# A hybrid encoder block on one core: up-projection of two chunks by seven block products in place of eight, behind the attention

## The chip, the core and the metric

The kernel runs on one core of a Trainium2 chip. The metric is the device time of one execution in microseconds (us); lower is better. TensorE (PE, with PEld for its weight loads) multiplies, VectorE (DVE), ScalarE (ACT) and GpSimd (POOL) do the elementwise work, and all transfers are issued from SyncE's queue (SP).

## What is computed

The reference takes x (2048 tokens of 1024 numbers, float32) through one encoder layer:

```python
hn = rms_norm(h, g_mix_pre)
u, q, k, v = split(hn @ w_in)                      # 512 wide each
mix = concat[pool_mixer(u), rms_norm(stick_breaking_attention(q, k, v)) * g_sb] @ w_out
h = h + rms_norm(mix, g_mix_post)
m = rms_norm(h, g_mlp_pre) @ w_up                  # 1024 -> 4096
m = square(relu(m)) @ w_down                       # 4096 -> 1024
h = h + rms_norm(m, g_mlp_post)
e = rms_norm(p @ w_ple_proj, g_ple)
h = h + sigmoid(h @ w_gate) * e
```

The attention is strictly causal: for each query, A = sigmoid(z) times the product of (1 - sigmoid(z)) over the keys between.

## The kernel before

**Tiling.** The tokens are cut into 4 chunks of 512. Activations lie feature-major: a tile has 128 features on the partitions and 512 tokens along the row. Every float32 operand of a product is split into a high part that PE reads exactly and a low rest (`split`, `pair`: an ACT copy and a DVE subtraction), and each product of 128 x 128 weights with 128 x 512 activations is three MATMULs (`mm3`): high by high, high by low, low by high. A weight tile is split at its first use and stored in DRAM as two halves; later chunks load those (`weight`, tiles `wh` and `wl`).

**Stages.** For each chunk: `ple` (p @ w_ple, its norm, tiles `e`), `prenorm`, `in_proj`, `u_proj` with `pool_mixer`, `attention`, `out_proj` with the residual (`output`), `feed_forward`, `gate`. The up-projection of one chunk (`mlp_ups`) makes 32 tiles of 128 hidden features, each from 8 x 3 MATMULs into one PSUM bank (tag `dn`); ACT takes the relu into `rl`, DVE squares it, and `pair` makes `m`. The down-projection (`mlp_downs`) takes two hidden tiles at a time (GF = 2): 8 output tiles of 6 MATMULs each (tag `dw`), which DVE adds into the page `acc`.

**Norms.** `add_square` squares a tile on ACT and adds it up on DVE (in `ple` on POOL) into `nrm`. `row_rstd` sums over the partitions with four small float32 matmuls against a column of ones (rows `nm<-ones,nrm`), makes the reciprocal root on POOL (`ms`), transposes it (`nm<-ident,rs`) and spreads it over the partitions by one more matmul (`nm<-rt,sel`).

**Attention.** A unit is one head and one pair of query and key chunk: 4 blocks of scores (`z`), two sigmoids on ACT (`q`, `pr`), a product scan on DVE (`q<-q,ones`), a product `pr<-pr,q` on POOL, 4 groups of transposes on PE (`tp`), their split (`at`: ACT and DVE), and 8 matmuls with the values (`op`). There are 80 units.

**Order.** The program is written twice. First the functions only record their operations, each with a due time: PE operations advance `plan.t`, the attention advances its own clock that runs `R_ATT` times as fast as its PE work. Then `Plan.order` simulates the engines with costs written by hand and fixes one order for each engine. On the chip each engine and the SP queue take their instructions in that order; what is late delays all that stands behind it. Buffers are 53 pages of SBUF and 8 PSUM banks.

**What runs beside what.** `attend` of chunks 0 to 3 is spread over the projections and the feed-forward of chunks 0, 1 and half of 2. `output(1)` is recorded within `feed_forward(0)`, `output(2)` within `feed_forward(1)`, `output(3)` within `feed_forward(2)`, `gate(0)` and `gate(1)` within `feed_forward(1)` and `(2)`. Behind `feed_forward(3)` come `gate(2)` and `gate(3)`. All recorded operations have the line of `Plan.record` (L275 in the profile), so rows are told apart by their tiles.

## Time and profile before

| | |
|---|---|
| median of 3 runs | 2663.43 us (2662.93 to 2663.47) |
| the profiled execution's own time | 2662.55 us |
| its span, first to last instruction | 2660.8 us |
| PE busy | 2626.7 us, 99% of the span |
| DVE / ACT / POOL busy | 64% / 39% / 27% |
| mean granted PE clock | 0.995 |
| moved by DMA | 668 MB, 251 GB/s |

PE's busy time is the first thing to look at, but its instructions are pipelined, so the time of a stretch is read from the distance of equal events in it, not from one instruction's duration. Idle time of an engine costs only where PE waits for it. In a group's row the mean duration of a DVE instruction contains what it waits for once it has started.

### The profile page before, as it was taken

Reading aid. Unit: us, or ns where it says so; the run is one execution under the profiler, and the core shown is the slowest. Engines: PE = TensorE matmul, PEld = TensorE weight load, DVE = VectorE, ACT = ScalarE, POOL = GpSimd, SP = SyncE. Lnnn points to the kernel's source line nnn. Section 1 sums busy time; section 2 is a strip of 40 time slices with the busy share of each in tenths; the row PEclk is TensorE's granted clock in tenths of the full one; section 3 lists DMA queues with packets and bytes.
Section 4 is the critical chain, followed back from the end, with each engine's and each line's share of the span. In section 5 each row is a group of like instructions: output and inputs, shape, how many; then the busy total and the mean of one; then the engine's idle time right before and its main releaser. Section 6 shows DMA issues by size and latency. Waiting matters only on the chain.

```text
span 2660.8 us, 34134 instructions
## 1 busy us (share of the span) xinstructions
PE 2626.7 (99%) x12312; PEld 2146.5 (81%) x12312; DVE 1709.8 (64%) x2331; ACT 1037.3 (39%) x1907; POOL 726.6 (27%) x663
## 2 busy tenths in 40 slices
PE   8999999999999999999999999999999999999999
PEld 6778787777888888888888888888887888888887
DVE  7854748868777759967665568685667273433454
ACT  8433536446445445445333343443334122111111
POOL 5432335344233323323333223333334000000000
PEclk9899999999999999999999999999999999999999
DMA  6899878878777758747955476475754675555576
GB/s 260 318 370 348 287 261 327 277 242 331 258 258 257 293 190 335 280 157 279 355 192 190 159 260 252 163 257 201 281 202 158 258 270 196 207 193 196 201 287 239
DMA packets 213129, 668.41 MB, mean 251 GB/s; under 512 B 22880, under 2 KB 39264, under 8 KB 212960
## 3 DMA queue, kind: packets, MB, share of 16 engines
q1 hardware_dynamic: 212960, 666.22, 69.8%
q8 instruction: 98, 1.61, 0.2%
q14 instruction: 71, 0.58, 0.1%
HBM read 489.97 MB, written 176.16 MB: 250 GB/s over the span
## 4 chain that ended last, share of the span: by engine, by line
PE 91%; DVE 4%; DMA 1%; ACT 1%; issue 1%; POOL 1%; SPq 0%; ACTq 0%; DVEq 0%; POOLq 0%
PE dn L275 50%; PE dw L275 26%; PE op L275 4%; PE z L275 4%; PE tp L275 4%; PE nm L275 2%; DVE q L275 1%; POOL nrm L275 1%; ACT nrm L275 1%; DMA wl<-d_w_up 0%; DMA d_y<-ypool 0%; DVE nrm L275 0%; DVE e L275 0%; DVE at L275 0%; POOL pt L275 0%
## 5 line engine op out<-in xcount | busy, mean ns | idle before, releaser
L275 PE MATMUL dn<-act,wh 128*128 128x512 f32 x2816 | 901.4, 401 | 4.3 <-ACT act L275 2.2
L275 POOL TENSOR_TENSOR pr<-pr,q 128x1 f32<-128x1 f32 (+4 forms) x512 | 564.5, 1115 | 1116.0 <-ACT pr L275 481.6
L275 PE MATMUL dw<-m,wh 128*128 128x512 f32 x2048 | 644.7, 396 | 3.0 <-DVE acc L275 3.0
L275 PEld LDWEIGHTS dn<-act,wh 128*128 128x128 f32 x2816 | 510.8, 190 | 103.0 <-issue 5.3
L275 PE MATMUL dn<-act,wl 128*128 128x512 f32 x1408 | 553.0, 393 | 0.0
L275 DVE TENSOR_TENSOR_SCAN q<-q,ones 128x512 f32<-128x512 f32 (+1 forms) x320 | 401.7, 1268 | 95.2 <-ACT q L275 94.0
L275 PEld LDWEIGHTS dw<-m,wh 128*128 128x128 f32 x2048 | 374.1, 188 | 76.3 <-DVE acc L275 3.4
L275 DVE TENSOR_TENSOR acc<-acc,dw 128x512 f32<-128x512 f32 x480 | 324.8, 681 | 139.1 <-PE dw L275 137.5
L275 PE MATMUL dw<-m,wl 128*128 128x512 f32 x1024 | 400.0, 391 | 0.0
L275 PEld LDWEIGHTS dn<-act,wl 128*128 128x128 f32 x1408 | 265.9, 189 | 57.8
L275 ACT CAST at<-tp 128x512 fp32r<-128x512 f32 (+1 forms) x320 | 166.5, 524 | 302.5 <-PE tp L275 271.9
L275 DVE TENSOR_TENSOR at<-tp,at 128x512 fp32r<-128x512 f32 (+1 forms) x320 | 191.1, 602 | 125.6 <-ACT at L275 125.2
L275 DVE TENSOR_TENSOR rl<-rl 128x512 f32<-128x512 f32 x128 | 97.7, 764 | 263.7 <-ACT rl L275 263.4
L275 ACT ACTIVATE q<-z 128x512 f32<-128x512 f32 (+1 forms) x320 | 171.3, 537 | 239.0 <-PE z L275 227.7
L275 ACT ACTIVATE rl<-dn 128x512 f32<-128x512 f32 x128 | 76.6, 598 | 472.3 <-PE dn L275 462.6
L275 PEld LDWEIGHTS dw<-m,wl 128*128 128x128 f32 x1024 | 192.2, 188 | 41.5
L275 POOL TENSOR_TENSOR ms<-ms,mhalf 128x4 f32<-128x4 f32 (+1 forms) x36 | 55.2, 1534 | 614.8 <-DVE ms L275 614.7
L275 PE MATMUL op<-at,kv 128*128 128x512 f32 (+3 forms) x640 | 182.9, 365 | 2.0 <-DVE at L275 2.0
L275 PE MATMUL z<-kv,qd 128*128 128x512 f32 (+3 forms) x640 | 178.1, 361 | 0.0
L275 ACT ACTIVATE pr<-z 128x512 f32<-128x512 f32 (+1 forms) x320 | 170.2, 534 | 5.2 <-PE op L275 2.6
L275 PE MATMUL tp<-ident,pr 128*128 128x128 f32 x1088 | 169.7, 272 | 1.2 <-DVE acc L275 0.6
L275 PEld LDWEIGHTS tp<-ident,pr 128*128 128x128 f32 x1088 | 136.0, 140 | 39.8 <-DVE acc L275 1.1
(118 smaller groups left out, 2961.7 us busy)
## 6 DMA issues: line engine op xcount, KB each, us to landing
wh<-d_w_up SPq DMA_DIRECT2D x96, 512.0 KB, 4.9
wl<-d_w_up SPq DMA_DIRECT2D x96, 512.0 KB, 6.0
wh<-d_w_down SPq DMA_DIRECT2D x96, 512.0 KB, 5.5
wl<-d_w_down SPq DMA_DIRECT2D x96, 512.0 KB, 5.2
xin<-d_h SPq DMA_DIRECT2D x48, 512.0 KB, 7.2
kv<-d_k SPq DMA_DIRECT2D x80, 256.0 KB, 6.1
kv<-d_v SPq DMA_DIRECT2D x80, 256.0 KB, 6.6
wh<-d_w_in SPq DMA_DIRECT2D x36, 512.0 KB, 8.1
```

What stands on the lines that cost most here:

```text
L275: fn(*[a.real() if isinstance(a, Ref) else a for a in args], **{k: a.real() if isinstance(a, Ref) else a for k, a in kw.items()})
```

## The change

`prenorm` no longer squares and adds the feature-major x. A second copy of x lies token-major in DRAM (`xr`, 4 tiles of 128 tokens x 1024 for each chunk); ACT squares each with a row sum (`token_sums`), so the four matmuls with ones go. In `ple` the sums move from POOL to DVE, and the scaling by gain and row norm moves to `gate`: the row norm is stored (`er`) and loaded there, and a gate tile takes three DVE operations in place of two. `output` of chunks 2 and 3 leaves the normalised activations unmade and hands on the row norm.

The feed-forward of chunks 2 and 3 is no longer interleaved with the attention. `output(2)` and `output(3)` lie within `feed_forward(1)`; then `moving_up` reads h1 of both chunks and makes 7 moving operands for each of 4 pairs of feature tiles (28 pages `xs`), beside `gate(0)`. `up_pair` then runs 16 times: it takes a 2 x 2 block (two halves of the features, two hidden tiles) against the 2 x 2 block (two halves of the features, two chunks), makes 4 sums of weights on DVE and splits them (`sa`, `so`), runs 7 products of 4 x 3 MATMULs and puts the four results together with one ACT copy and 7 DVE additions (`pu`, `mo`). The results are stored in DRAM and read back by `down_pair`, which takes both chunks and four hidden tiles at a time (GD = 4). `gate(1)`, `gate(2)`, `gate(3)` come last. The planner's numbers are others, and PE operations that read another engine's result are planned 2 us later (`MARGIN`).

```diff
+    def token_sums(self, rows):
+        sums = self.plan.tile([P, 16], F32, "ms")
+        for b in range(4):
+            t = self.plan.tile([P, D], F32, "xr")
...
+                self.sp.dma_start(out=t, in_=rows[b])
+            self.act.activation(t, t, AF.Square, accum_out=sums[:, b:b + 1])
...
+    def prenorm(self, dram, rows, which):
+        rs = self.rstd(self.token_sums(rows), 4, D)
         ts = [self.load2(dram, k2, "xp") for k2 in range(4)]
-        nrm = None
-        for k in range(NK):
-            nrm = self.add_square(nrm, ts[k // 2][:, k % 2, :])
-        r = self.row_rstd(nrm)
...
+            bank = self.spread(rs, self.bank("nm"))
...
-            nrm = self.add_square(nrm, m, self.pool)
-        r = self.row_rstd(nrm)
...
+            nrm = self.add_square(nrm, m)
...
+        self.sp.dma_start(out=dd["er"][c], in_=self.row_rstd(nrm))
...
+    def moving(self, k, b11, b12, b21, b22):
...
+        sub(t1, b12, b11)
+        sub(t2, b22, t1)
+        sub(t3, b22, b12)
+        sub(t4, b21, t2)
+        return [self.pair("xs", t) for t in (b11, b21, b22, t4, t1, t2, t3)]
...
+    def stationary_up(self, b, w_up, kept):
...
+        add(s1, a21, a22, ALU.add)
+        add(s2, s1, a11, ALU.subtract)
+        add(s3, a11, a21, ALU.subtract)
...
+        add(s4, a12, s2, ALU.subtract)
+        sums = [self.pair("so", t) for t in (s4, s1, s2, s3)]
...
+    def block(self, ws, xs, done):
...
+        p1 = mul(0)
...
+        self.act.copy(hold, p1)
+        u2 = add(hold, mul(5))
+        add(hold, mul(1), 0, 0)
+        u3 = add(u2, mul(6))
+        p5 = mul(4)
+        u4 = add(u2, p5)
+        add(u3, p5, 1, 1)
+        add(u4, mul(2), 0, 1)
+        add(u3, mul(3), 1, 0)
...
+    def down_pair(self, gi, accs, w_down, dd):
...
+            self.sp.dma_start(out=t, in_=dd["m"][gi * GD + j])
+            for i in range(2):
+                ms[i].append(self.pair("m", t[:, i, :]))
+        units = [self.weight(w_down[gi * GD + j], dd["w_down"][gi * GD + j], False) for j in range(GD)]
...
-                self.dve.tensor_tensor(out=s, in0=s, in1=ge[i][:, j, :], op=ALU.mult)
+                self.dve.scalar_tensor_tensor(out=s, in0=s, scalar=self.g(G_PLE, ot), in1=ge[i][:, j, :], op0=ALU.mult,
+                                              op1=ALU.mult)
+                self.dve.tensor_tensor(out=s, in0=s, in1=rows[i], op=ALU.mult)
                 self.dve.tensor_tensor(out=h, in0=h, in1=s, op=ALU.add)
...
-        feed_forward(1, ((G_GATE, gate, 0), (G_OUT, output, 2)))
-        feed_forward(2, ((G_GATE, gate, 1), (G_OUT, output, 3)))
+        feed_forward(1, ((G_OUT2, output, 2), (G_OUT3, output, 3)))
         plan.rate = 1.0
-        feed_forward(3, ())
+        xs = net.moving_up(2, 3, [acts[2], acts[3]])
+        gate(0)
+        for b in range(NF // 2):
+            net.up_pair(b, xs, w_up, dd)
+        accs = [[], []]
+        for gi in range(NF // GD):
+            net.down_pair(gi, accs, w_down, dd)
+        net.mlp_post(2, accs[0], dd)
+        net.mlp_post(3, accs[1], dd)
+        gate(1)
         gate(2)
-        plan.t += T_END
         gate(3)
-R_ATT = 4.515
+R_ATT = 3.117
+MARGIN = 2.0
...
-                        o.ready = max(o.ready, pick.end + LATENCY[e][o.engine])
+                        late = MARGIN if o.engine == "pe" and e != "pe" else 0.0
+                        o.ready = max(o.ready, pick.end + LATENCY[e][o.engine] + late)
```

What the change makes of the order is seen on three places. The first is PE at the program's start, where `pl` is the product p @ w_ple, `nm` a norm and `dn` the input projection. Before:

```order
L275 MATMUL pl<-pp,plew 128x512 x96
L275 MATMUL nm<-ones_76,nrm 128x1 x4
L275 MATMUL pl<-pp,plew 128x512 x6
L275 MATMUL nm<-ones_76,nrm 128x1 x4
L275 MATMUL pl<-pp,plew 128x512 x9
L275 MATMUL nm<-ident,rs 8x128
L275 MATMUL pl<-pp,plew 128x512 x6
L275 MATMUL nm<-rt,sel_92 128x512
```

The same place now:

```order
L279 MATMUL pl<-pp,plew 128x512 x48
L279 MATMUL nm<-ident,rs 8x128
L279 MATMUL pl<-pp,plew 128x512 x15
L279 MATMUL nm<-rt,sel_92 128x512
L279 MATMUL pl<-pp,plew 128x512 x12
L279 MATMUL nm<-ident,rs 8x128
L279 MATMUL pl<-pp,plew 128x512 x15
L279 MATMUL nm<-rt,sel_92 128x512
L279 MATMUL pl<-pp,plew 128x512 x36
L279 MATMUL nm<-ones_76,nrm 128x1 x4
```

The norms of x stand without their matmuls with ones and 48 `pl` MATMULs earlier; the first norm of `ple` now stands behind 126 of them.

The second is PE where the first gate (`dn<-actg`) begins; numbers tell the buffers apart. Before it stands among attention units (`z`, `tp`, `op`) and an up-projection (`dn<-act`):

```order
L275 MATMUL z_11528<-maskb_134,identb_129 128x128
L275 MATMUL dn_11484<-act_10252,wh_11152 128x512 x2
L275 MATMUL dn_11484<-act_10252,wl_11157 128x512
L275 MATMUL tp_11537<-ident_71,pr_11195 128x128 x2
L275 MATMUL tp_11537<-ident_71,pr_11244 128x128 x2
L275 MATMUL dn_11484<-act_10263,wh_11152 128x512 x2
L275 MATMUL dn_11484<-act_10263,wl_11157 128x512
L275 MATMUL op_11100<-at_11504,kv_10734 128x512 x2
L275 MATMUL dn_11484<-act_10274,wh_11152 128x512 x2
L275 MATMUL dn_11484<-act_10274,wl_11157 128x512
L275 MATMUL dn_11561<-actg_11404,wh_11393 128x512 x2
```

Now no attention is left there, and the end of that gate runs into the first of the seven products (`dn<-xs`):

```order
L279 MATMUL dn_17145<-actg_16825,wh_16957 128x512 x2
L279 MATMUL dn_17145<-actg_16825,wl_16970 128x512
L279 MATMUL nm_17134<-rt_17189,sel4_92 128x512
L279 MATMUL dn_17145<-actg_16835,wh_16957 128x512 x2
L279 MATMUL dn_17145<-actg_16835,wl_16970 128x512
L279 MATMUL dn_17193<-xs_17036,wh_16858 128x512 x2
L279 MATMUL dn_17193<-xs_17036,wl_16865 128x512
L279 MATMUL dn_17235<-xs_17113,so_17132 128x512 x3
L279 MATMUL dn_17193<-xs_17055,wh_16858 128x512 x2
L279 MATMUL dn_17193<-xs_17055,wl_16865 128x512
```

So the 16 blocks stand behind all of the attention, and between the last statistics of chunk 3 and the first products lies little but that gate.

The third is DVE within the up-projection. Before, two hidden tiles of one chunk, with the additions of a down-projection behind them:

```order
L275 TENSOR_TENSOR rl_21332<-rl_21332 128x512
L275 TENSOR_TENSOR m_21348<-rl_21332,m_21348 128x512
L275 TENSOR_TENSOR rl_21356<-rl_21356 128x512
L275 TENSOR_TENSOR acc_20063<-acc_20063,dw_21336 128x512
L275 TENSOR_TENSOR m_21368<-rl_21356,m_21368 128x512
```

Now a part of one block, with the weight sums of a later one among it:

```order
L279 TENSOR_TENSOR pu_18389<-pu_18354,dn_18363 128x512
L279 TENSOR_TENSOR mo_18401<-pu_18354,dn_18329 128x512
L279 TENSOR_TENSOR so_18393<-sa_18320,so_18393 128x512
L279 TENSOR_TENSOR sa_18411<-ws_18132 128x512
L279 TENSOR_TENSOR pu_18389<-pu_18389,dn_18373 128x512
L279 TENSOR_TENSOR sa_18411<-sa_18411,ws_18135 128x512
L279 TENSOR_TENSOR mo_18401<-mo_18401 128x512
L279 TENSOR_TENSOR pu_18354<-pu_18389,dn_18395 128x512
L279 TENSOR_TENSOR mo_18443<-pu_18389,dn_18395 128x512
```

DVE there reads products from PSUM (`dn`) itself, and nothing of a down-projection stands between.

## Rows read from the trace of the kernel before

**Rows 1.** Page, parts 1 and 2: busy time; granted PE clock in 40 slices.
```profile
PE 2626.7 (99%) x12312; PEld 2146.5 (81%) x12312; DVE 1709.8 (64%) x2331; ACT 1037.3 (39%) x1907; POOL 726.6 (27%) x663
PEclk9899999999999999999999999999999999999999
```
**Rows 2.** Busy time by stretch; columns as in the first line.
```profile
core 0: us, PE busy (x) PEld busy (x) DVE busy (x) ACT busy (x) POOL busy (x), PEclk, DMA share, GB/s
0.00:133.00 133.00, 119.10 (x503) 94.50 (x504) 103.46 (x141) 83.45 (x141) 63.35 (x81) 0.95 0.78 289
133.00:2045.00 1912.00, 1896.94 (x9098) 1548.56 (x9097) 1334.07 (x1766) 843.91 (x1582) 656.83 (x577) 1.00 0.72 255
2062.00:2570.00 508.00, 508.00 (x2252) 418.98 (x2251) 223.78 (x350) 89.42 (x149) 5.04 (x4) 1.00 0.63 230
...
997.80:1130.80 133.00, 133.00 (x646) 108.84 (x645) 123.83 (x171) 68.05 (x122) 47.85 (x43) 1.00 0.84 308
```
**Rows 3.** ACT in order of time in chunk 3's feed-forward: start, duration, what, idle before.
```profile
2500.29 0.60 ACT L275 ACTIVATE rl<-dn 128x512 f32<-128x512 f32 x1 [17.74 <-PE dn L275]
...
2522.05 0.60 ACT L275 ACTIVATE rl<-dn 128x512 f32<-128x512 f32 x1 [17.74 <-PE dn L275]
...
2543.81 0.60 ACT L275 ACTIVATE rl<-dn 128x512 f32<-128x512 f32 x1 [16.11 <-PE dn L275]
```
**Rows 4.** PE in order of time: the partition sums of one norm.
```profile
2578.98 0.95 PE L275 MATMUL nm<-ones,nrm 128*128 128x1 f32 x8
2579.78 0.72 PE L275 MATMUL dn<-actg,wh 128*128 128x512 f32 x2
```
**Rows 5.** Who PE waited for in the whole span: us, times, longest.
```profile
PE pl L275 <- ACT plew L275: 6.9, 1, 6.9
PE nm L275 <- DVE rt L275: 5.9, 2, 3.6
PE dw L275 <- DVE acc L275: 3.0, 1, 3.0
```
**Rows 6.** Stretches in which PE's clock was granted at 0.50.
```profile
74.90:85.10 10.20, 9.65 (x26) 7.67 (x27) 9.01 (x12) 7.21 (x11) 6.63 (x4) 0.50 0.93 339
98.80:102.20 3.40, 3.40 (x9) 2.63 (x10) 2.74 (x4) 1.06 (x2) 0.00 (x0) 0.50 0.73 222
289.90:296.70 6.80, 6.08 (x15) 4.72 (x16) 6.80 (x12) 3.77 (x9) 0.00 (x0) 0.50 0.21 77
419.70:423.10 3.40, 3.40 (x12) 2.90 (x12) 2.48 (x3) 2.93 (x7) 3.40 (x4) 0.51 0.94 272
```
**Rows 7.** Groups by form: POOL's sums of squares in `ple`: busy, mean ns, idle before.
```profile
L275 POOL TENSOR_TENSOR nrm<-nrm 128x512 f32<-128x512 f32 x28 | 51.9, 1870 | 37.2 <-ACT nrm L275 37.2
```
**Rows 8.** Groups by form: the scan, two additions on DVE, the product on POOL.
```profile
L275 POOL TENSOR_TENSOR pr<-pr,q 128x511 f32<-128x511 f32 x224 | 337.0, 1507 | 490.6 <-DVE q L275 296.4 <-ACT pr L275 52.1 <-ACT q L275 35.5
L275 DVE TENSOR_TENSOR_SCAN q<-q,ones 128x512 f32<-128x512 f32 x224 | 325.7, 1463 | 81.2 <-ACT q L275 80.8 <-issue 0.2
L275 DVE TENSOR_TENSOR acc<-acc,dw 128x512 f32<-128x512 f32 x480 | 324.8, 681 | 139.1 <-PE dw L275 137.5
```
**Rows 9.** All engines in order of time, near the attention's end.
```profile
2026.48 11.40 POOL L275 TENSOR_TENSOR pr<-pr,q 128x511 f32<-128x511 f32 x9
2027.52 4.39 DVE L275 TENSOR_TENSOR_SCAN q<-q,ones 128x512 f32<-128x512 f32 x2
...
2031.83 1.25 DVE L275 TENSOR_TENSOR acc<-acc,dw 128x512 f32<-128x512 f32 x2
...
2032.54 0.73 PE L275 MATMUL dw<-m,wh 128*128 128x512 f32 x2 [2.99 <-DVE acc L275]
```
**Rows 10.** DVE in order of time at the program's end: one gate tile.
```profile
2654.32 0.69 DVE L275 TENSOR_TENSOR gs<-gs,geh 128x512 f32<-128x512 f32 x1 [6.07 <-ACT gs L275]
...
2655.05 0.69 DVE L275 TENSOR_TENSOR geh<-geh,gs 128x512 f32<-128x512 f32 x1
```
**Rows 11.** Busy time of the stretch in which DMA was densest.
```profile
133.00:266.00 133.00, 132.65 (x631) 107.36 (x629) 68.57 (x106) 50.45 (x104) 35.36 (x33) 1.00 1.04 359
```

More of the change, by code (lines that the diff above doesn't have):

```diff
@@ new lines, in moving_up, with part, half @@
+    def moving_up(self, c, d, rows):
+        got = []
+        for k2 in range(2):
+            low, high = self.both(c, d, k2, rows), self.both(c, d, k2 + 2, rows)
+            for j in range(2):
+                got.append(self.moving(k2, low[0][:, j, :], low[1][:, j, :], high[0][:, j, :], high[1][:, j, :]))
+        return [[g[i] for g in got] for i in range(7)]
+    def stationary_up(self, b, w_up, kept):
+        raw = [self.plan.tile([P, D], F32, "ws") for _ in range(2)]
+        for t, i in zip(raw, (2 * b, 2 * b + 1)):
+            self.sp.dma_start(out=t, in_=w_up[i])
+        first = [self.plan.tile([P, D], F32R, t) for t in ("wh", "wl")]
+        other = self.page("wo", F32R)
+        for a in range(2):
+            self.sp.dma_start(out=first[a].as_(F32), in_=kept[2 * b][a])
+            self.sp.dma_start(out=other[:, a, :].as_(F32), in_=kept[2 * b + 1][a][:, CH:D])
+        a11, a12 = raw[0][:, 0:CH], raw[0][:, CH:D]
+        a21, a22 = raw[1][:, 0:CH], raw[1][:, CH:D]
+        add = lambda out, a, b, op: self.dve.tensor_tensor(out=out, in0=a, in1=b, op=op)
+        ss, us = self.page("sa"), self.page("sa")
+        s1, s2, s3 = ss[:, 0, :], ss[:, 1, :], us[:, 0, :]
+        add(s1, a21, a22, ALU.add)
+        add(s2, s1, a11, ALU.subtract)
+        add(s3, a11, a21, ALU.subtract)
+        s4 = us[:, 1, :]
+        add(s4, a12, s2, ALU.subtract)
+        sums = [self.pair("so", t) for t in (s4, s1, s2, s3)]
+        def part(t):
+            return [(t[:, 0, i * P:(i + 1) * P], t[:, 1, i * P:(i + 1) * P]) for i in range(4)]
+        def half(lo):
+            return [(first[0][:, lo + i * P:lo + (i + 1) * P], first[1][:, lo + i * P:lo + (i + 1) * P])
+                    for i in range(4)]
+        return [half(0), half(CH), part(sums[0]), part(other), part(sums[1]), part(sums[2]), part(sums[3])]
@@ new lines, in product, with add @@
+    def product(self, w, x):
+        bank = self.bank("dn")
+        self.mm3(bank, [(lh, ll, t[:, 0, :], t[:, 1, :]) for (lh, ll), t in zip(w, x)])
+        return bank
+    def block(self, ws, xs, done):
+        mul = lambda i: self.product(ws[i], xs[i])
+        def add(a, b, o=None, t=None):
+            out = sums.pop(0) if o is None else outs[o][:, t, :]
+            self.dve.tensor_tensor(out=out, in0=a, in1=b, op=ALU.add)
+            if o is not None:
+                done(o, t, out)
+            return out
+        outs = [self.page("mo") for _ in range(2)]
+        pages = [self.page("pu") for _ in range(2)]
+        sums = [pages[0][:, 0, :], pages[0][:, 1, :], pages[1][:, 0, :]]
+        p1 = mul(0)
+        hold = pages[1][:, 1, :]
+        self.act.copy(hold, p1)
[7 more added lines that the diff above has]
+        add(u3, mul(3), 1, 0)
+        return outs
@@ new lines, in up_pair, with square @@
+    def up_pair(self, b, xs, w_up, dd):
+        def square(o, t, r):
+            self.act.activation(r, r, AF.Relu)
+            self.dve.tensor_tensor(out=r, in0=r, in1=r, op=ALU.mult)
+        outs = self.block(self.stationary_up(b, w_up, dd["w_up"]), xs, square)
+        for o in range(2):
+            self.sp.dma_start(out=dd["m"][2 * b + o], in_=outs[o])
+    def down_pair(self, gi, accs, w_down, dd):
+        ms = [[], []]
+        for j in range(GD):
+            t = self.page("mi")
+            self.sp.dma_start(out=t, in_=dd["m"][gi * GD + j])
+            for i in range(2):
+                ms[i].append(self.pair("m", t[:, i, :]))
+        units = [self.weight(w_down[gi * GD + j], dd["w_down"][gi * GD + j], False) for j in range(GD)]
+        for i in range(2):
+            for ot in range(NK):
+                ps = self.bank("dw")
+                cs = slice(ot * P, (ot + 1) * P)
+                self.mm3(ps, [(units[j][0][:, cs], units[j][1][:, cs], ms[i][j][:, 0, :], ms[i][j][:, 1, :])
+                              for j in range(GD)])
+                if gi == 0:
+                    if ot % 2 == 0:
+                        accs[i].append(self.page("acc"))
+                    self.act.copy(accs[i][-1][:, ot % 2, :], ps)
+                else:
+                    a = accs[i][ot // 2][:, ot % 2, :]
+                    self.dve.tensor_tensor(out=a, in0=a, in1=ps, op=ALU.add)
@@ L955, in gate @@
     def gate(self, cs, acts, w_gate, dd, out, first):
+        rows = []
+        for c in cs:
+            rows.append(self.page("er")[:, 0, :])
+            self.sp.dma_start(out=rows[-1], in_=dd["er"][c])
         for ot in range(NK):
@@ L999, in build @@
                 dd[n].append(dram(f"{n}{c}", [P, NK, CH]))
+            dd["er"].append(dram(f"er{c}", [P, CH]))
+        dd["m"] = [dram(f"m{f}", [P, 2, CH]) for f in range(NF)]
+        net.h1 = dd["h1"]
         for n, m in (("w_in", 12), ("w_v", 4), ("w_out", NK), ("w_up", NF), ("w_down", NF), ("w_gate", NK)):
```

66 lines of the change are left out of this document (42 added, 24 removed).

## The prediction

> **What bounds the kernel now.** The first view is the page: PE is busy 99% of the span at a granted clock of nine tenths or more in all 40 slices but one, and but for PE's own weight loads no other is over 64% [rows 1]. The second, busy time by stretch, says where PE is not busy [rows 2]: 13.9 us are lost in the first 133 us (6.9 of them before the first weights are there [rows 5]), 15.1 us in the 1912 us with the attention, none in the 508 us behind it. The third, the waits, names the releasers: rt, a step of a norm, 5.9 us in two waits; a DVE addition, 3.0 us [rows 5]. The fourth, the stretches with a granted clock of 0.50, adds what a wait leaves behind: 23.8 us at half speed, 13.6 of them early [rows 6]. PE's own work is the bound, and little else can be had.
>
> What a MATMUL costs is read from equal events: in chunk 3's feed-forward the same relu returns every 21.76 us [rows 3]; between two of them lie two up tiles of 24 and eight down tiles of 6 MATMULs, 96 in all: 0.2267 us each.
>
> **The change, part by part.** The sum is made against the profiled execution's own 2662.55 us, 0.9 below the median of the three runs.
>
> *Seven products for eight.* Eight products of 12 MATMULs in each of 16 blocks become seven: 16 x 12 = 192 fewer, 192 x 0.2267 = **43.5 us**. They go from a stretch in which PE waits for nothing [rows 2], so all of it lies on the path.
>
> *Norms of x.* Four norms lose their sums over the partitions. One takes 0.80 us (2578.98 to 2579.78, eight records for four float32 matmuls) [rows 4]: **3.2 us**.
>
> *The start.* Early loss that could go is 5.9 us of waits for rt [rows 5] and half of 13.6 us at half clock [rows 6]: 12.7 us. In these 133 us POOL is busy for 63 us [rows 2], much of it sums of squares at 1.87 us that stand before norms [rows 7]; on DVE an addition takes 0.68 us [rows 8]. The order moves the norms of x in front of the others. Against it: the eight copies of x that come first are 4.2 MB, 11.7 us at 359 GB/s [rows 11], and x itself waits behind them; 126 `pl` MATMULs (28.6 us) stand before the first projection and cover that. I take half, **-6.4 us**; bounds -12.7 and +5.
>
> *The attention, compressed.* Between the first and last score matmul the lists now hold 2006 fewer 512-wide MATMULs, 455 us: about 1457 us for the same 80 units in place of 1912, 18.2 us a unit and not 23.9. DVE loses there 126 `acc` additions, 64 for hidden tiles, 48 of gates and some 70 others, 308 in all: 209 us at 0.68 [rows 8], and with what they wait for beside POOL I take 230. So it is busy for about 1104 us, 76% where it was 70%; POOL keeps some 645 of its 657 us and goes from 34% to 44%. The nearest stretch, 997.8 to 1130.8 us, had DVE at 93% and POOL at 36% while PE was busy for all of its 133.0 us [rows 2]. So I price the density at nothing. The loss there now is 15.1 us of idle PE and half of 10.2 us at half clock: 20.2 us. Bounds: all of it goes (the planner now leaves PE 2 us of margin), or it doubles: -20.2 and +20.2.
>
> One row speaks against that. Near 2027 us POOL multiplies nine times without a pause, two scans beside it take 4.39 us in place of two times 1.46 [rows 8, 9], the addition behind them is late, and PE waits 2.99 us [rows 9]. The Trainium skill ("SBUF — State Buffer", section "SBUF: two separate sides") has a rule for it: a DVE instruction with two SBUF inputs and a GpSimd instruction that reads SBUF take one shared pair of ports, and whichever starts second waits for the whole of the other. These rows agree with it. By that rule the 326 us of wide scans and POOL's 645 us exclude each other, 67% of the stretch where it was 51%; more such waits would follow. That is the second rival.
>
> *The edge before the blocks.* This is new: nothing but `gate(0)` lies between the last statistics of chunk 3 and the products that need all 28 `xs`. In DVE's list 140 instructions stand between that norm's rt and the last `xs` that the first block reads, eight of them 1024 wide, so 148 units of 512. In PE's list 387 wide MATMULs and a norm's small ones stand between the same two points: 88.9 us. A DVE unit costs 0.57 (two additions in 1.25 us, one in 0.68 [rows 8, 9]) to 0.68 us: 84 to 101 us. PE is either just covered or waits 12 us. Transfers are as tight: from the last weight of `feed_forward(1)` to the first of the second block the queue issues 31.7 MB, 88 us at 359 GB/s, over 72 us of PE work; at that rate and a DMA share of 1.04 PE was busy for 132.65 of 133 us [rows 11]. A wait of 3 us can bring a stretch of 3.4 us at half clock, 1.7 us lost [rows 6]. I take **+4 us**, near the covered end, by the 0.57 us at which DVE goes through instructions that wait for nothing; bounds 0 and +16.
>
> *Blocks and down-projection.* A block is 84 MATMULs, 19.0 us, beside 19 DVE instructions (12.9 us), 9 of ACT (5.4 us at 0.60 [rows 3]) and 3.7 MB, 193 GB/s. A down group is 192 MATMULs, 43.5 us, beside 24 DVE instructions (16 us). PE waited for nothing at 230 GB/s [rows 2], so 0. If the cover went, DVE would have to be half as slow again.
>
> *The end.* Three gates stand together now. From the last gate weight of chunk 1 on, 37.8 MB are issued ahead of the last weight, over 86 us of PE work: 440 GB/s where 359 is the most seen [rows 11], so 7 MB have to come early, into pages that the down-projection has left. I take **+2 us**; bounds 0 and +12. Behind the last matmul one more dependent DVE instruction stands, 0.73 us (2654.32 to 2655.05 [rows 10]): **+0.7 us**.
>
> The sum: 2662.55 - 43.5 - 3.2 - 6.4 + 0 + 4 + 2 + 0.7 = 2616.2. I predict **2616 us**, a gain of 1.8%.
>
> **The rivals.**
>
> *First: the new order is clean.* The margin does what it says: the early waits go, the edge is covered, and three quarters of the attention's loss vanishes. 2662.55 - 43.5 - 3.2 - 12.7 - 15.2 + 0.7 = 2589. For it: 508 us without any wait [rows 2] show that a plan of this kind can be kept. Against: the attention has less time, not more.
>
> *Second, on the other side: POOL and DVE hold each other up in the attention.* The mechanism is that of rows 9, with the price of rows 9: 3.0 us of PE each time that POOL runs without a pause beside the scans. The time without it is 2616; slower by over 0.2% begins at 2668, 52 us later. That takes 17 such waits, or 0.65 us in each of the 80 units. Before there was one of this size in 80. At 76% of DVE and 44% of POOL a few more are likely, 17 are not; five would give 2631.
>
> *Third: the changeovers cost what their upper bounds say.* Edge +16, end +12, no gain at the start: 2662.55 - 46.7 + 16 + 12 + 0.7 = 2645. For it: three sums above have no slack (DVE, transfers at the edge, transfers at the end). Against: transfers can run ahead, and the bounds take each at its worst.
>
> *Fourth: the change does not save its MATMULs,* because what hangs on a product (its bank, its reader, its sums of weights) costs PE time each time. All of the 43.5 us is lost again if each of the 112 products waits 0.39 us: 2660. Against: 8 banks and DVE at 68% of a block leave room.
>
> **How the numbers follow.** Forecast 2616 (2605 to 2628): 0.50. First rival, 2589 (to 2605): 0.20. Third, 2645 (from 2628): 0.19, with the smaller forms of the second in it. Second, over 2668: 0.05. Fourth: 0.03; left over for no change in other ways: 0.03. The range that leaves out 2 in 10 reaches from 2592 to 2648. About 0.2%, 5.3 us, is what a measurement of this kernel can tell from no change: faster 0.90, within it 0.04, slower 0.06.
>
> **What would show it.** The page of the changed kernel should hold 192 fewer 512-wide MATMULs and PE busy near 99%. A block should take 19.0 us from relu group to relu group; more says that DVE or a transfer is late there. The two early waits for rt and the half clock at 75 us should be gone or shorter. In the attention, scans should take about 1.46 us and POOL's products 1.51; a mean scan near 2.2 us, with PE waiting for `acc` or `at`, is the second rival. Waits of PE for `xs`, or for a `wh` by DMA, just behind `gate(0)` show the edge; waits for `wh` or `actg` in the last 100 us show the end. The prediction is wrong if the attention's stretch loses more than some 40 us of PE time, or if the edge or the end loses more than 15.

## The result and the profile after

The changed kernel takes **2619.66 us** (median of four runs, 2619.36 to 2620.76) where the kernel before takes 2663.18 us: a ratio of 0.9839 with a 95% interval of 0.9822 to 0.9856, a gain of 43.5 us. The forecast was 2616. The profiled execution took 2619.36 us, 43.2 less than the one before.

Part 1 of the page after; it answers to [rows 1]:

```profile
PE 2578.0 (98%) x12088; PEld 2106.5 (80%) x12088; DVE 1781.9 (68%) x2471; ACT 1070.2 (41%) x1999; POOL 683.4 (26%) x635
```

PE has 224 records fewer: the 192 MATMULs of the eighth products and 32 of four norms (eight each [rows 4]). It is busy for 48.7 us less and idle for 39.6 us of the span where it was for 34.1.

Busy time by stretch after, as in [rows 2]; the stretches are the start, the attention, the edge before the blocks, the blocks, the down-projection, the gates, and last the first third of the attention by itself:

```profile
core 0: us, PE busy (x) PEld busy (x) DVE busy (x) ACT busy (x) POOL busy (x), PEclk, DMA share, GB/s
0.00:133.00 133.00, 125.61 (x551) 100.71 (x552) 72.72 (x123) 79.14 (x136) 10.21 (x54) 1.00 0.99 380
133.00:1600.00 1467.00, 1448.21 (x7117) 1179.11 (x7116) 1155.14 (x1471) 760.18 (x1463) 665.26 (x575) 0.99 0.73 253
...
1805.00:1840.00 35.00, 30.29 (x126) 24.15 (x125) 32.04 (x52) 17.15 (x32) 0.00 (x0) 0.95 0.51 172
1840.00:2110.00 270.00, 270.00 (x1191) 223.18 (x1190) 184.11 (x295) 77.33 (x135) 0.00 (x0) 1.00 0.59 214
2110.00:2472.00 362.00, 362.00 (x1599) 299.85 (x1598) 137.30 (x212) 57.58 (x104) 0.00 (x0) 1.00 0.50 187
2472.00:2560.00 88.00, 85.23 (x371) 68.57 (x370) 55.15 (x92) 19.12 (x34) 2.90 (x2) 0.98 0.93 351
...
160.00:660.00 500.00, 485.68 (x2407) 392.35 (x2406) 374.85 (x501) 272.43 (x559) 243.30 (x204) 0.98 0.85 292
```

The early loss has shrunk from 13.9 us to 7.4. The attention loses 18.8 us in 1467 where it lost 15.1 in 1912, 14.3 of them between 160 and 660 us. The edge loses 4.7, the gates 2.8; the 205 us between attention and edge, the blocks and the down-projection lose nothing.

Who PE waited for, in the whole span (us, times, longest), to be set beside [rows 5]:

```profile
PE op L279 <- DVE at L279: 7.8, 8, 2.8
PE pl L279 <- ACT plew L279: 6.9, 1, 6.9
PE dn L279 <- DVE xs L279: 4.7, 1, 4.7
PE z L279 <- DVE at L279: 3.4, 2, 2.6
PE dn L279 <- DVE actg L279: 1.5, 2, 1.0
PE dn L279 <- ACT actg L279: 1.3, 1, 1.3
```

The first weights (`plew`) are as late as before; the early waits for rt and the one for a down-projection's `acc` are gone (norms still wait 4.1 us for rs, 0.5 of it early). In their place stand `at`, the split of the attention's weights, then `xs` at the edge and `actg` at the end.

The stretches with a granted clock of 0.50 after, as in [rows 6]:

```profile
283.90:294.10 10.20, 7.89 (x21) 6.12 (x22) 8.95 (x14) 4.75 (x11) 4.41 (x4) 0.50 0.49 140
423.90:427.30 3.40, 3.40 (x11) 2.94 (x10) 3.40 (x5) 0.00 (x0) 3.40 (x3) 0.50 0.00 0
638.90:642.30 3.40, 3.12 (x7) 2.51 (x8) 2.71 (x6) 2.54 (x6) 0.00 (x0) 0.50 0.97 313
1833.60:1837.00 3.40, 2.98 (x7) 2.41 (x8) 3.40 (x7) 1.04 (x2) 0.00 (x0) 0.50 0.91 275
2523.10:2526.50 3.40, 3.40 (x9) 2.67 (x8) 3.40 (x6) 1.14 (x2) 0.00 (x0) 0.50 1.02 416
```

It is 23.8 us again, but none of it early: 17.0 us lie in the attention, 3.4 behind the wait for xs, 3.4 behind the wait for actg.

### The profile page after: what moved, and what is told of

Its sections match the earlier page's. It is cut to its first block, busy times and chain, and to the rows that moved or that the text cites. A ratio compares the mean times of both kernels' runs of the same rounds, so it can differ in the third digit from the quotient of the medians.

```text
span 2617.6 us, 33833 instructions
## 1 busy us (share of the span) xinstructions
PE 2578.0 (98%) x12088; PEld 2106.5 (80%) x12088; DVE 1781.9 (68%) x2471; ACT 1070.2 (41%) x1999; POOL 683.4 (26%) x635
## 5 line engine op out<-in xcount | busy, mean ns | idle before, releaser
L279 POOL TENSOR_TENSOR pr<-pr,q 128x511 f32<-128x511 f32 (+4 forms) x512 | 573.3, 1137 | 710.3 <-ACT pr L279 281.2
L279 PE MATMUL dn<-act,wh 128*128 128x512 f32 x1792 | 577.6, 403 | 0.0
L279 DVE TENSOR_TENSOR acc<-acc,dw 128x512 f32<-128x512 f32 x352 | 237.7, 682 | 237.8 <-PE dw L279 236.8
L279 PEld LDWEIGHTS dn<-act,wh 128*128 128x128 f32 x1792 | 319.7, 190 | 57.9 <-issue 3.2
L279 PE MATMUL dn<-act,wl 128*128 128x512 f32 x896 | 351.9, 393 | 0.0
L279 ACT CAST at<-tp 128x512 fp32r<-128x512 f32 (+2 forms) x320 | 167.5, 530 | 186.6 <-PE tp L279 164.5
L279 DVE TENSOR_TENSOR at<-tp,at 128x512 fp32r<-128x512 f32 (+2 forms) x320 | 189.2, 597 | 48.7 <-ACT at L279 48.1
L279 PEld LDWEIGHTS dn<-act,wl 128*128 128x128 f32 x896 | 168.8, 188 | 37.4
L279 PE MATMUL dn<-xs,so 128*128 128x512 f32 x768 | 191.8, 389 | 0.0
L279 PEld LDWEIGHTS dn<-xs,so 128*128 128x128 f32 x768 | 144.1, 188 | 30.5 <-DVE so L279 0.5
```

What stands on the lines that cost most here:

```text
L279: fn(*[a.real() if isinstance(a, Ref) else a for a in args], **{k: a.real() if isinstance(a, Ref) else a for k, a in kw.items()})
```

## Experiments

All times stand against the changed kernel's 2619.66 us. Where an edit says "order kept", the planner sees the old cost, so every engine's list stays the same and only the instruction's width changes. Most results are the median of two executions; thirteen executions of the kernel before spread from 2661.27 to 2665.95 us, so a difference of 2 or 3 us decides nothing.

### The seven products undone

```diff
-        return [self.pair("xs", t) for t in (b11, b21, b22, t4, t1, t2, t3)]
+        return [self.pair("xs", t) for t in (b11, b21, b12, b22)]
...
-        outs = self.block(self.stationary_up(b, w_up, dd["w_up"]), xs, square)
+        for o in range(2):
+            wh, wl = self.weight(w_up[2 * b + o], dd["w_up"][2 * b + o], False)
+            for t in range(2):
+                bank = self.bank("dn")
+                moving = xs[2 * t] + xs[2 * t + 1]
+                self.mm3(bank, ...)
```

> The changed kernel with the seven products undone and nothing else: in the same 16 places of the program each hidden tile of each chunk is made by plain products again (8 of 12 MATMULs in a block of two hidden tiles and two chunks, moving operands are the split h1 itself), so no sums of weights, no sums of h1, no additions behind the products. Base is the changed kernel's 2619.66 us. Theory (PE bounds the blocks, their sums lie beside its work): 192 more MATMULs x 0.2267 = +43.5 us; the wait of 4.7 us before the blocks with its 1.7 us at half clock may go, as DVE makes fewer operands: 2657 to 2663. Rival (the sums cost PE time, or the gain comes from moving the stage behind the attention): below 2645.

Measured: 2659.23 us (three rounds), 39.6 more. Part 1 of its page, and the waits in which it differs:

```profile
PE 2618.7 (99%) x12280; PEld 2141.3 (81%) x12280; DVE 1617.2 (61%) x2203; ACT 1018.4 (38%) x1907; POOL 682.2 (26%) x635
```
```profile
PE dn L279 <- DVE actg L279: 2.3, 1, 2.3
PE dn L279 <- ACT actg L279: 2.0, 1, 2.0
```

PE is busy for 40.7 us more with 192 MATMULs more, and no wait for xs is left. The loss at the edge (4.7 us and 1.7 for the half clock) goes, the one at the end grows by 3.2 (waits for actg of 4.3 us in place of 2.8, half clock 6.8 in place of 3.4): 43.5 - 6.4 + 3.2 = 40.3. The theory holds: the products are worth their PE time, and the sums around them cost PE nothing but the edge. Against the kernel before this one stands at 0.9986 (0.9977 to 0.9996): all the rest of the change together, without the products, is worth 4 us.

### What took the early loss away

Three parts of the change could have done it. Each was undone alone.

```diff
-        rs = self.rstd(self.token_sums(rows), 4, D)
...
+        nrm = None
+        for k in range(NK):
+            nrm = self.add_square(nrm, ts[k // 2][:, k % 2, :])
+        r = self.row_rstd(nrm)
```

> The changed kernel with the x row sums undone: x is squared feature-major on ACT, added up on DVE and summed over the partitions by PE, as in the kernel before. The sums of the other norm stay on DVE, the planner's margin stays. Theory 1 (the row sums took the early loss away): the four norms' sums over the partitions cost 3.2 us, and the early loss of the first 133 us comes back, PE idle 13 to 14 us there in place of 7.4 and a stretch of 10 us at half clock: 2619.7 + 3.2 + 13.3 = 2636. Rival (the margin, or the sums that left POOL, took it away): PE idle in the first 133 us stays below 9 us, 2619.7 + 3.2 = 2623.

```diff
-            nrm = self.add_square(nrm, m)
+            nrm = self.add_square(nrm, m, self.pool)
```

> The changed kernel with one thing undone: the sums of squares of the p norms (28 additions in ple) go back from DVE to POOL, where one took 1.87 us. Theory 1 (row sums took the early loss away): no change, 2619.7 within 2 us, PE idle in the first 133 us stays near 7.4. Rival (it was POOL's sums ahead of the norms): POOL is busy for over 55 us of the first 133 in place of 10, PE idle there comes back to 13 us with half clock: 2628 to 2633.

```diff
-MARGIN = 2.0
+MARGIN = 0.0
```

> The changed kernel with MARGIN 0 in place of 2.0: the planner lets PE's operations stand as early as another engine's result is due. Theory 1 (row sums took the early loss away, the margin is a trifle there): PE idle in the first 133 us stays below 9 us. In the attention, where PE now idles 18.8 us between 133 and 1600 us, more waits for at, pr and acc: 25 to 40 us, total 2625 to 2640. Rival (the margin took the early loss away): PE idle in the first 133 us is 12 us or more.

Measured: 2627.74 us without the row sums (+8.1), 2627.83 with the p norms' sums on POOL (+8.2), 2638.06 without the margin (+18.4). The first 133 us of the three, in this order (columns as above):

```profile
0.00:133.00 133.00, 126.06 (x560) 101.49 (x561) 90.36 (x150) 84.29 (x144) 12.50 (x54) 1.00 1.00 380
```
```profile
0.00:133.00 133.00, 120.00 (x519) 95.59 (x520) 66.84 (x89) 79.04 (x134) 53.06 (x81) 0.99 0.99 378
```
```profile
0.00:133.00 133.00, 126.17 (x552) 101.31 (x553) 72.87 (x124) 79.51 (x137) 10.14 (x54) 1.00 0.99 384
```

Only the second gives the early idle time back: 13.0 us, with POOL busy for 53 us and not 10. So the idle time went with the p norms' sums that left POOL, not with the row sums and not with the margin; theory 1 fell. The half clock is another matter: of the 13.6 us early in the kernel before, the second run shows 3.4 again (from 51.8 us), the other two none. So 7.3 us of the early gain (5.6 of idle time and half of 3.4) are shown to be POOL's sums; which part of the change, or which together, took the rest of the half clock away is not shown. The row sums' 8.1 us do not lie early. 3.2 us of them are the norms' matmuls; PE is idle for 1.4 us more in the span; the remaining 3.5 us I can't assign. The margin's 18.4 us lie in many places, some 15 of them in the attention (idle 28.4 us in place of 18.8 between 133 and 1600 us, half clock 27.3 in place of 17.0). The stretch with the u projections beside it:

```profile
160.00:660.00 500.00, 479.91 (x2361) 386.63 (x2361) 368.79 (x495) 267.16 (x545) 228.87 (x198) 0.97 0.84 284
```

PE is idle there for 20.1 us and not 14.3, and its waits for `at` before the products with the values (`op`) are 12.1 us in the span, not 7.8. One caution: the planner's other numbers are those of the changed kernel, so a part undone runs in a plan that was not set for it.

### The attention: POOL's window sums, or its products

The waits between 160 and 660 us lie where the u projections run beside the units. One of these places in the changed kernel, all engines in order of time:

```profile
281.52 3.46 POOL L279 TENSOR_TENSOR pr<-pr,q 128x511 f32<-128x511 f32 x1
...
283.76 1.24 DVE L279 TENSOR_TENSOR rs<-ms,rs 128x8 f32<-128x8 f32 x1
284.95 1.27 POOL L279 TENSOR_TENSOR pt<-pt 128x513 f32<-128x513 f32 x1
285.06 0.38 PE L279 MATMUL nm<-ident,rs 128*16 128x128 f32 x1 [2.55 <-DVE rs L279]
...
286.25 1.47 DVE L279 SCALAR_TENSOR_TENSOR pt<-pt,u 128x512 f32<-128x512 f32 x1 [1.25 <-POOL pt L279]
...
287.65 0.55 DVE L279 TENSOR_TENSOR at<-tp,at 128x384 fp32r<-128x384 f32 x1
...
288.25 0.69 PE L279 MATMUL op<-at,kv 128*128 128x384 f32 x1 [1.15 <-DVE at L279]
```

A product takes 3.46 us on POOL in place of 1.5 [rows 8] and ends at 284.98 us. A norm's subtraction on DVE (`rs<-ms,rs`, 8 columns) takes 1.24 us beside it and ends at 285.00; PE waits 2.55 us for that, its longest wait here. The next window sum (`pt<-pt`) starts only behind the product; DVE's `pt<-pt,u` waits 1.25 us for that and takes 1.47; the split `at` stands behind it in DVE's queue; PE waits for `at`. Two edits, order kept:

```diff
-            self.pool.tensor_tensor(out=nx[:, 0:width], in0=..., in1=..., op=ALU.add)
+            self.pool.tensor_tensor(out=nx[:, 0:width], in0=..., in1=..., op=ALU.add, only=32, swap=...)
```

> The changed kernel in its own order, but POOL's window sums of the pool mixer (40 additions of 1.1 to 1.5 us, all before 640 us) write 32 columns in place of some 520; their readers take the unsummed u, so the mixer's result is left out. In the changed kernel PE idles 14.3 of the 18.8 us that it loses in the attention between 160 and 660 us, where the u projections of chunks 1 to 3 run beside the units, and 17 us at half clock follow. Theory A (there the window sums stand among the attention's products on POOL, and DVE's instruction that waits for a window sum holds up the splits `at` behind it): idle from 160 to 660 us falls below 6 us, half clock at 284 and 639 us goes: 2619.7 - 8 - 7 = 2605. Rival B (the density of scans and POOL products over the whole attention does it): idle there stays over 11 us, 2616 to 2620.

```diff
-            self.pool.tensor_tensor(out=pr[:, 1:W], in0=pr[:, 1:W], in1=q[:, 0:W - 1], op=ALU.mult)
+            self.pool.tensor_tensor(out=pr[:, 1:W], in0=pr[:, 1:W], in1=q[:, 0:W - 1], op=ALU.mult, only=32)
```

> The changed kernel in its own order, but each of POOL's wide products in the attention (320, 1.56 us for 511 columns) makes 32 columns; the rest of the product is left out. Theory B (POOL's products and DVE's work hold each other up): scans of 512 columns fall from a mean of 1.44 us to 1.25 or less, PE idle from 133 to 1600 us falls from 18.8 to below 5 us and the 17 us at half clock there go: 2619.7 - 14 - 8 = 2598. Theory A (window sums, not products) and rival C (DVE's and ACT's own work in order, whatever POOL does): scans get short as well, but idle from 160 to 660 us stays over 8 us and the time over 2608.

Measured: 2608.95 us (-10.7) and 2600.78 us (-18.9). The stretch from 160 to 660 us with short window sums:

```profile
160.00:660.00 500.00, 492.65 (x2464) 398.53 (x2462) 371.55 (x511) 278.93 (x570) 223.79 (x210) 0.99 0.87 299
```

With short products, the attention's stretch and the scans:

```profile
133.00:1600.00 1467.00, 1460.45 (x7203) 1193.40 (x7203) 1051.72 (x1482) 765.27 (x1469) 341.69 (x575) 1.00 0.74 257
```
```profile
L281 DVE TENSOR_TENSOR_SCAN q<-q,ones 128x512 f32<-128x512 f32 x224 | 282.1, 1273 | 75.1 <-ACT q L281 74.1
```

In the stretch from 160 to 660 us both do nearly the same: short window sums take PE's idle time there from 14.3 to 7.4 us, short products to 6.6. Behind it, from 660 to 1600 us, 4.5 us were lost; short window sums leave them, short products take them all. Neither theory holds alone: window sums and products share POOL, and taking either away frees the chain. Theory A was near on its own edit (7.4 where it wanted under 6), but it also said that short products would not help in that stretch, and they do. Theory B fits the time of its edit within 3 us, with both its bounds just missed (scans at 1.27 us where it wanted 1.25, idle 6.6 where it wanted under 5), and not that of the first. Whether the loss is mostly DVE held up by POOL, or POOL late, these two don't separate, since both edits make POOL faster. The next edit takes the window sums off POOL as well, but gives their work to DVE.

```diff
-            self.pool.tensor_tensor(out=nx[:, 0:width], in0=..., in1=..., op=ALU.add)
+            self.dve.tensor_tensor(out=nx[:, 0:width], in0=..., in1=..., op=ALU.add)
```

> The changed kernel with nothing left out, the 40 window sums of the pool mixer on DVE in place of POOL. Theory A1 (what costs is that DVE waits in its queue for POOL's chain of window sums, which stands among the products): a window sum of 0.7 us on DVE takes less than the chain's wait, idle of PE from 160 to 660 us falls from 14.3 to 9 or less, 2611 to 2616. Rival A2 (what costs is work on the engine that also makes the splits: 27 us more on DVE, which is busy for 375 of those 500 us, and its two SBUF inputs beside POOL's products): idle stays or grows, 2619 to 2630.

Measured: 2614.21 us (-5.5). The same stretch:

```profile
160.00:660.00 500.00, 489.47 (x2434) 396.01 (x2434) 379.18 (x536) 278.69 (x565) 211.71 (x178) 0.99 0.86 296
```

DVE does 35 instructions more in this stretch, 30 of them window sums of 21.8 us in all, and is busy for only 4.3 us more: its other instructions have become shorter, by some 19 us together (the 13 splits `ypool<-pt,ypool` from a mean of 1.14 to 0.88 us, the eight subtractions `rs<-ms,rs` on 128x8 from 0.60 to 0.29). So that much of DVE's busy time had been waiting for POOL. PE's idle time falls to 10.5 us. A1 holds in sign and time, not quite in its bound of 9 us. How much of the rest is POOL late with its own work stays open.

### The edge before the blocks

```diff
-        sub = lambda out, a, b: self.dve.tensor_tensor(out=out, in0=a, in1=b, op=ALU.subtract)
+        sub = lambda out, a, b: self.dve.tensor_tensor(out=out, in0=a, in1=b, op=ALU.subtract, only=32, swap=...)
```

> The changed kernel in its own order, but the 16 subtractions that make the moving sums of h1 write 32 columns in place of 512, and the operands are split from h1 itself; the sums are left out. That takes some 9 us of DVE work from in front of the last operand that the first block reads. Theory (DVE is late there, as its row says): the 4.7 us wait for xs at 1829 us and the 3.4 us at half clock behind it go: 2619.7 - 6.4 = 2613. Rival (transfers of h1 or of the weights set that point): a wait of over 3 us stays there, 2617 or more.

Measured: 2620.01 us. The wait for xs is 3.7 us where it was 4.7, and the half clock behind it stays. The theory fell: 9 us of DVE work less in front of that wait shorten it by 1. Twelve of the 16 subtractions stand ahead of a point at which DVE itself waits for PE, a step (`rt`) of chunk 1's norm. There DVE's wait only grows; first the changed kernel, then this run:

```profile
1808.71 0.68 DVE L279 TENSOR_TENSOR rt<-nm,pick 8x512 fp32r<-8x512 f32 x1 [2.09 <-PE nm L279]
```
```profile
1810.27 0.68 DVE L281 TENSOR_TENSOR rt<-nm,pick 8x512 fp32r<-8x512 f32 x1 [3.09 <-PE nm L281]
```

Behind that point four subtractions are left, and what they give, 2 us, goes in part into waits for ACT. What DVE does later there in the changed kernel, and PE, in order of time:

```profile
1827.37 5.38 DVE L279 SCALAR_TENSOR_TENSOR acc<-acc,gains,nrm 128x512 f32<-128x512 f32 x8
1832.67 0.69 DVE L279 TENSOR_TENSOR xt<-xin,xt 128x512 f32<-128x512 f32 x1
1833.27 0.69 DVE L279 TENSOR_TENSOR xs<-xt,xs 128x512 fp32r<-128x512 f32 x1
...
1834.02 1.22 PE L279 MATMUL dn<-xs,wo 128*128 128x512 f32 x2 [4.71 <-DVE xs L279]
```

Eight scalings of chunk 1's result, wanted by nobody before `gate(1)` some 600 us later, stand in one row ahead of the last subtraction that the block needs. The next edit makes these eight short, order kept:

```diff
-        self.residual(acc, G_MPOST, self.row_rstd(nrm), dd["h1"][c], dd["h2"][c])
+        self.residual(acc, G_MPOST, self.row_rstd(nrm), dd["h1"][c], dd["h2"][c], only=32 if c == 1 else None)
```

> The changed kernel in its own order, but the eight scalings of chunk 1's down-projection result (`acc<-acc,gains,nrm` in mlp_post(1), 0.67 us each) make 32 columns in place of 512; that part of chunk 1's result is left out. They stand in one row in DVE's queue from 1827.4 to 1832.7 us, ahead of the subtraction of the last xs that the first block reads, and nobody needs them before the gates at the end. Theory (these eight are the wait before the blocks: 8 x 0.6 = 4.8 us against the 4.7 us that PE waits): the wait and the 3.4 us at half clock behind it go, 2619.7 - 6.4 = 2613. Rival (the number of operands, or ACT's casts behind the sigmoids of gate(0), sets it): a wait of over 2.5 us stays, 2616 or more.

Measured: 2621.11 us (2620.10 and 2622.11). PE's waits at that place, in order of time:

```profile
1830.43 0.73 PE L281 MATMUL dn<-xs,wo 128*128 128x512 f32 x2 [0.71 <-DVE xs L281]
1833.59 0.77 PE L281 MATMUL dn<-xs,wh 128*128 128x512 f32 x2 [2.43 <-DMA wh<-d_w_up]
1834.86 0.80 PE L281 MATMUL dn<-xs,wl 128*128 128x512 f32 x1 [0.50 <-DMA wl<-d_w_up]
```

The cause named is right and the time is not: the wait for xs falls from 4.7 to 0.7 us, but PE then runs into the next block's weights, which come 2.4 and 0.5 us too late (issued at 1827.2 and 1827.9 us). 3.6 us of idle time and the half clock stay. The rival's time came in, but not by its causes, the operands' number or ACT's casts. Two limits lie there, 1 us apart.

### The end

```diff
+            if gi == NF // GD - 1:
+                self.mlp_post(2 + i, accs[i], dd)
...
-        net.mlp_post(2, accs[0], dd)
-        net.mlp_post(3, accs[1], dd)
```

> The changed kernel with chunk 2's norm, residual and store recorded between the two halves of the last down group, some 21.7 us earlier in the plan than now, where they stand behind both halves; nothing is left out. Theory (the loss at the end is a planned lateness: chunk 2's last addition is done at 2457 us, its norm's sums run at 2484, the residual ends at 2509 and the first operand of its gate is split at 2520, 1.3 us too late): the 2.8 us of waits for actg and the 3.4 us at half clock go, 2619.7 - 4.5 = 2615. Rival (transfers are the limit there, 37.8 MB in front of the last weight): the wait stays or turns into one for a weight, 2618 or more.

Measured: 2623.47 us, 3.8 slower. The waits for actg are 4.3 us in place of 2.8, and the half clock there 6.8 in place of 3.4. The edit did not move the norm: the first of the two norms has its sums on PE at 2486.1 us, 2484.3 in the changed kernel, and why the earlier entry in the plan had no effect I can't read from the runs. So this run doesn't decide on transfers. In the changed kernel ACT, DVE and PE at that place read:

```profile
2519.16 0.58 ACT L279 COPY nrm<-nm 128x512 f32<-128x512 f32 x1
2519.63 1.15 ACT L279 CAST actg<-xin 128x512 fp32r<-128x512 f32 x2
...
2519.78 1.41 DVE L279 SCALAR_TENSOR_TENSOR acc<-acc,gains,nrm 128x512 f32<-128x512 f32 x2 [3.19 <-ACT nrm L279]
...
2520.31 0.50 PE L279 MATMUL dn<-actg,wh 128*128 128x512 f32 x1 [1.25 <-ACT actg L279]
...
2521.11 1.29 DVE L279 TENSOR_TENSOR actg<-xin,actg 128x512 fp32r<-128x512 f32 x2
...
2521.85 0.50 PE L279 MATMUL dn<-actg,wh 128*128 128x512 f32 x1 [1.03 <-DVE actg L279]
```

It is the edge's pattern again, in two queues. ACT's cast of the first operand for chunk 2's gate stands behind the copy of chunk 3's row norm, and DVE's split of it behind two of chunk 3's scalings, for which DVE has waited 3.19 us; with post_early five of them stand there. PE waits first for the one, then for the other. So the norms' places were changed, both at the edge and at the end:

```diff
+            late.append((c, accs[0]))
...
             net.up_pair(b, xs, w_up, dd)
+            if b == 2:
+                net.mlp_post(*late.pop(), dd)
...
-        net.mlp_post(2, accs[0], dd)
-        net.mlp_post(3, accs[1], dd)
+        net.mlp_post(2, accs[0], dd, (10.0, NORM_LAG[1]))
+        net.mlp_post(3, accs[1], dd, (10.0, NORM_LAG[1]))
```

> The changed kernel with nothing left out, planned otherwise in two places: chunk 1's norm, residual and store (mlp_post(1)) are recorded behind the third block in place of before the operands xs, and the norms of chunks 2 and 3 behind the down-projection are due 10 us after their sums in place of 34. Theory (both late places are DVE's queue: scalings that nobody waits for stand ahead of splits that PE waits for): the wait for xs with its half clock goes (-6.4), the waits for actg and their half clock at 2520 us go (-4.5): 2609. Rival (transfers set the end, the operands' number the edge): no wait less, 2616 to 2624.

Measured: 2612.56 us (-7.1). Its gates' stretch, and the one wait that is left at the edge:

```profile
2472.00:2560.00 88.00, 88.00 (x395) 72.07 (x394) 52.05 (x88) 16.82 (x30) 2.35 (x2) 1.00 0.92 359
```
```profile
PE dn L279 <- DVE xs L279: 2.9, 6, 0.9
```

The end loses nothing now, at 359 GB/s: transfers were not the limit there. At the edge six short waits of 2.9 us in all stay, without half clock. By place the edge gives back 3.5 us and the end 4.5 (idle time and half of the half clock); the two edits were not run apart.

### Both edits that gave something

```diff
-            self.pool.tensor_tensor(out=nx[:, 0:width], in0=..., in1=..., op=ALU.add)
+            self.dve.tensor_tensor(out=nx[:, 0:width], in0=..., in1=..., op=ALU.add)
```

This is late_post with the window sums on DVE.

> The changed kernel with nothing left out and both edits that gave something alone: late_post's places for the norms (2612.6 us, -7.1) and the 40 window sums on DVE (2614.2 us, -5.5). Theory (they act in different stretches, 1800 to 2560 us and 160 to 660 us, and PE bounds all else): the two add up, 2619.7 - 7.1 - 5.5 = 2607, and PE idle from 160 to 660 us is 9 to 11 us. Rival (the new places let DVE run later in a stretch that the window sums load): only one of the two is left, 2612 to 2615.

Measured: **2606.93 us** over five rounds (2604.92 to 2607.40), a ratio to the kernel before of 0.9789 (0.9775 to 0.9802). The two add up as expected; with this it is faster than both kernels. PE's idle time in the stretch of the u projections is 11.9 us, somewhat over the 9 to 11 expected:

```profile
160.00:660.00 500.00, 488.12 (x2432) 395.00 (x2431) 379.38 (x535) 278.68 (x565) 209.50 (x178) 0.99 0.86 296
```

## Why the prediction was right, and where it was not

The time was 3.7 us above the forecast. The terms, from the two profiles (idle time of PE, and half of a change in half clock):

| term | predicted | measured | how |
|---|---|---|---|
| seven products | -43.5 | about -42 | PE busy 40.7 us more in eight_plain, with 3.4 us less half clock |
| norms of x | -3.2 | not measured apart | 32 records gone; -3.2 stands in the sum |
| start | -6.4 | -13.3 | idle 13.9 to 7.4, half clock 13.6 to 0 |
| attention | 0 | +7.1 | idle 15.1 to 18.8, half clock 10.2 to 17.0 |
| edge | +4 | +6.4 | idle 4.7, half clock 3.4 |
| end, gates | +2 | +4.5 | idle 2.8, half clock 3.4 |
| end, last instruction | +0.7 | +0.8 | idle of the last 21 us 5.1 to 5.9 |

With 43.5 for the products and 3.2 for the norms of x the measured column sums to -41.2, against the -43.2 of the two profiled executions; 2 us I do not assign. That the time came within 4 us is in part luck: the start gave 6.9 us more than its term and the attention took 7.1 more than its own, and the two cancel; edge and end took 4.9 more together.

**The main term is shown.** From one `pu<-dn` of ACT to the second next it is two blocks:

```profile
1918.76 0.59 ACT L279 COPY pu<-dn 128x512 f32<-128x512 f32 x1 [1.53 <-PE dn L279]
...
1956.84 0.59 ACT L279 COPY pu<-dn 128x512 f32<-128x512 f32 x1 [1.53 <-PE dn L279]
```

That is 19.04 us a block where 19.0 was predicted; two down groups start 43.52 us apart (43.5). PE waits for nothing in either stretch, and eight_plain gives the time back. The fourth rival fell with it.

**The start was mis-sized, and its reason was wrong.** I took half of the loss because I saw the gain in the norms of x standing first. Undoing that part leaves the start as it is. What brings the early idle time back is another part of the change: the p norms' sums, 1.87 us each on POOL [rows 7], went to DVE. The prediction had that row and named it, but drew only the order from it. pool_sums accounts for 7.3 of the 13.3 us; the other 6 are mostly half clock that no single part brings back. The gain lies just outside the bound of -12.7.

**The attention's zero was the optimistic side of its own bounds.** It rested on a stretch without a single u projection [rows 2, from 997.8 us]. The kernel before already lost most in the other kind of stretch, 10.4 of its 15.1 us:

```profile
160.00:620.00 460.00, 449.58 (x2177) 362.23 (x2176) 312.09 (x438) 228.70 (x455) 180.99 (x152) 0.99 0.85 298
620.00:2045.00 1425.00, 1420.36 (x6806) 1164.39 (x6805) 1007.81 (x1304) 611.03 (x1121) 472.64 (x422) 1.00 0.67 239
```

The changed kernel does so too: 14.3 of 18.8 us where POOL's window sums stand among its products. The mechanism is close to that of the second rival, DVE held up by POOL (window_sums_dve), and its rate was right in kind (waits of up to 2.8 us, the forecast of "a few more"): the loss grew by 7 us, not by the 52 that the rival needed. The mean scan came out at 1.44 us, near the 1.46 predicted for the case without it, so that mean is no test: the waits hang on a few places, not on the average. The margin of 2 us, which I weighed only as a reason for a gain, is what held the loss down: without it the kernel is 18.4 us slower, some 15 of them in the attention.

The Trainium skill ("SBUF — State Buffer", section "SBUF: two separate sides") says that a DVE instruction with two SBUF inputs and a GpSimd instruction that reads SBUF exclude each other for their whole duration. The rows agree: the product that starts at 281.52 us takes 3.46 us, and the DVE subtraction on 128x8 that starts at 283.76, and takes 0.17 us at 313.65, takes 1.24 and ends 0.02 us behind the product.

**The edge was right in place and nearly in size, wrong in its limit.** I counted DVE's instructions ahead of the last xs, took their number as the price, and let DVE go through them without a wait. In the trace it waits among them, 2.09 us for PE at 1808.7 us, so moving_sums_32 takes 9 us of that work away and gains 1 us of the wait. What counts is what stands behind the last such wait: there, eight scalings of another chunk, 5.4 us, and right behind them transfers, which the prediction had named as equally tight. That transfers were near is shown by scalings_32.

**The end was priced for the wrong reason.** I divided bytes by time and found 440 GB/s needed where 359 was seen; that 359 is a mean over 133 us, and the same page has a slice of 66.5 us at 370. late_post runs the same gates at 359 GB/s without a wait: the weights come early enough. The loss lay in the queues of ACT and DVE: late_post has both row norms copied by 2495.7 us and chunk 3's eight scalings done by 2510.2, ahead of the first cast for chunk 2's gate at 2510.3 and the first split at 2513.9, and PE does not wait.

**Of the rivals**, the clean order (2589) asked for three quarters of the attention's loss and no edge; late_post_dve, 18 us above it, shows that the end can be had, the edge mostly and the attention only in part. The third rival (2645) took bounds that did not come: edge and end cost 11 us and not 28.

## What to carry to other kernels

Undone one at a time, the products, the row sums, the POOL sums and the margin are worth 39.6, 8.1, 8.2 and 18.4 us, 74 in all, while the whole change gained 43.5; with the products undone the rest was worth 4 us. The four values do not add up, because each is taken with the other three in place: the margin, for one, holds down a loss in the attention that the change itself makes. The denser attention and the new edges cost 18 us by the table (7.1, 6.4 and 4.5); the rest of the difference is not assigned. A PE saving is kept only where the order around it is paid for. At a changeover, find the last point at which the late engine itself waits, look at which instructions stand between it and the one that is waited for, and ask who needs them; the number of instructions and the bytes per second come after that. Sums that one engine does slowly are best judged by the stretch with the most kinds of work on it, not by the densest one of a single kind.

## What the runs showed of the hardware that was not expected

DVE's busy time is no measure of its work while POOL runs beside it: 35 more instructions, 30 of them sums of 21.8 us in all, raised it by 4.3 us in a stretch of 500 us when POOL lost the same sums. The DMA queues moved 380 GB/s over the first 133 us and 416 GB/s in the 3.4 us from 2523.1 us, above the 359 that the prediction took as the most seen (and the 370 of one slice of the page before). Waits of 2.8 us in three pieces, the longest 1.3, were followed by a stretch at half clock at the end (2523.1 us); late_post's six waits of 2.9 us in all, none above 0.9, were not.
